# The first up-projection weights split during the last output products, and the last residual queued behind the first sums

## Chip, cores and metric

The kernel runs on one core of one Trainium2 chip. The metric is device time in microseconds (us); lower is better. A core has TensorE (PE in the profile, its weight loads PEld), VectorE (DVE), ScalarE (ACT), GpSimd (POOL) and SyncE (SP), which issues most of the DMAs. Each engine works off its own queue in order.

## What is computed

One inference step of a trunk of two layers, over 512 latent tokens and 128 context tokens of width 1024, in float32. Layer 0 mixes tokens by two-dimensional neighbourhood attention, layer 1 by grouped-query attention. After each mixer comes a gated convolutional feed-forward network (FFN). The parts around the change are these:

```python
xs = xs + g_as * rmsnorm(os_.reshape(bs, ts, -1) @ w_o, norm_mix_post[l])    # output products, residual
hs = rmsnorm(xs, norm_ffn_pre[l]) * (1.0 + sc_fs) + sh_fs                     # norm, scale and shift
fs = conv_ffn(hs, ffn_w_up[l], ffn_conv_w[l], ffn_conv_b[l], ffn_w_down[l])

def conv_ffn(h, w_up, conv_w, conv_b, w_down):
    u = h @ w_up                                            # 1024 -> 2 x 2816
    up = jnp.pad(u, ((0, 0), (1, 1), (0, 0)))
    u = up[:, :-2] * conv_w[0] + up[:, 1:-1] * conv_w[1] + up[:, 2:] * conv_w[2] + conv_b
    a, gt = jnp.split(u, 2, axis=-1)
    return (jax.nn.silu(a) * gt) @ w_down
```

The context tokens go the same way with their own g, sc and sh.

## The kernel before

**Numbers.** A float32 operand is split into a rounded high part (a copy on ACT) and a low part, the difference (a subtraction on DVE or POOL). A product is three matmuls: high with high, low with high, high with low. A weight goes through three kinds of buffers in the pool `wp`, four of each: `wr` (as loaded), `wh` and `wl` (its parts). A buffer is used again when its last reader is done, so a load or a split waits for that.

**Tiles.** The 640 tokens are five tiles of 128; tile 4 is the context. The output projection of the mixer (class `Mix`, from line 659) runs in two halves of 512 columns. `part0` makes the first halves `y0` of all tiles ahead; `second` (line 675) goes through the tiles and makes the second half `y1`, eight products (p = 0 to 7) per tile, with the four weights `ws[1, 0]` to `ws[1, 3]`, each for two values of p. Within the products of tile t, behind p = TP = 1, it issues the transposes of tile t-2, and the residual and the shift of tile t-1.

**Finish** (class from line 318) turns products into the FFN's input. `ahead` loads the modulation rows (`mod`) and the old residual (`xo`). `stat` squares and sums half a row on ACT (line 349) and lets POOL scale the sum (351); `rms` takes the power on POOL (358). `sums` multiplies the products by the gate on DVE (366 and 368) and gives the banks of the products back. `residual` adds to the old residual on DVE (378, two halves), stores it, takes squares again and multiplies by the norm's scale (387, two halves). `shifted` applies the root and the shift on DVE (393, two halves). `turns` transposes the tile on TensorE (117); the results are copied into `hF` and, for the first columns, split into the parts `B` (215, 216 on ACT, 220 on DVE).

**The FFN's beginning** (`ffn`, line 1063). The up-projection has 22 pairs of chunks, the value and the gate of 128 features. Most pairs are multiplied by a scheme that forms sums of blocks of the weights (lines 1132 to 1135) and of the columns (class `Halves`, line 194) and saves products. The first `PLAIN` = 2 pairs, four chunks, go the plain way, since the column sums are not there yet. `plain0` (line 1229) makes two products of twelve matmuls for one chunk, `ux` and `uy`, over the first 322 columns, which are ready first. It copies `ux` on ACT (1165), adds `uy` to the copy on DVE (1236) into the tile `C`, and gives the bank of `uy` back. `plain1` does the other columns later. Between the `plain0` of the second and the third chunk stand the transposes of tile 3, behind the fourth those of tile 4; then follow the two products of the next value weight, and `plain1` of the four chunks. `Halves.first` (line 233) makes column parts from `hF` (237 on DVE, 230 on ACT, 231 on DVE). `fetch` (1103) loads up to four weights ahead, one more for each that has been split; `split` makes the parts (1111 on ACT, 1112 on DVE or POOL). The low parts of the first two chunks are on POOL, those of the other two on DVE.

**The order.** TensorE's order is that of the program text (the helper `pe` chains its instructions). PSUM has eight banks, which the class `Banks` hands out first in, first out. On the other engines a planner at build time orders the instructions: what is traced first has the higher rank, and what it takes to be ready and ranks highest comes next. Each engine then keeps that order, whatever really is ready. An explicit edge (`tc.add_manual_dep`) fixes the order of two instructions.

Of the kernel before, what the change touches and what calls it, by code (L numbers as in the profile page):

```python
# [101 lines left out]
def hybrid_step(ctx: ExitStack, tc: tile.TileContext, A, O):  # L102
# [215 lines left out]
    class Finish:  # L318
# [27 lines left out]
        def stat(self, y, first=None):  # L346
            junk = self.np.tile([P, 512], BF16, tag="junk", name="junk")
            ss = sm.tile([P, 1], F32, name="sso", bufs=12)
            nc.scalar.activation(junk, y, AF.Square, accum_out=ss)
# [23 lines left out]
        def residual(self, t):  # L373

            xm, r = self.xm[t]
            xo = self.xo.pop(t)
            for c in HALF:
                nc.vector.scalar_tensor_tensor(xo[:, c], xm[:, c], r, xo[:, c], op0=ALU.mult, op1=ALU.add)
                if not self.nxt:
                    nc.sync.dma_start(self.xnew(t)[:, c], xo[:, c])  # L380
            if not self.nxt:
                return
            nc.sync.dma_start(self.xnew(t), xo)
            v = None
            for c in HALF:
                v = self.stat(xo[:, c], v)
                (nc.vector if v else nc.gpsimd).tensor_mul(xm[:, c], xo[:, c], self.gs[:, c])
            self.xm[t] = xm, self.rms(v)

        def shifted(self, t):  # L390
            xm, r = self.xm[t]
            for c in HALF:
                nc.vector.scalar_tensor_tensor(
                    xm[:, c], xm[:, c], r, self.sh[:, c], op0=ALU.mult, op1=ALU.add
                )

        def turns(self, t):
# [259 lines left out]


    class Mix:

# [13 lines left out]

        def second(self, fin):

# [377 lines left out]
    for t in range(NT):  # L1054
        m0.part0(t, 7)
    late = m0.second(fin)
    fin.close()
    r_na.close()
# [3 lines left out]

    def ffn(l, hT, hT_close, xold, xnew, nxt, todo, late, late_close, side, back, after=None):

# [27 lines left out]
        with ExitStack() as s2:  # L1092
            sw = s2.enter_context(pool("sw", 1, side))
            sw2 = s2.enter_context(pool("sw2", 2, side))
            ct = up = ada = None
            ws, raws, done = {}, {}, set()
            nr = [0]

# [64 lines left out]
            def copied(name, p, u):  # L1163
                small[name, p] = sw2.tile([P, TH], F32, tag=name, name=name)
                nc.scalar.copy(small[name, p], u)  # L1165

# [62 lines left out]
            def plain0(p, i):  # L1229

                x = banks["p", p, i] = bk.get("ux")
                block_product(x[:, 0:TH], ws[p, i], 0, "11", True)
                copied("c1", (p, i), x[:, 0:TH])
                y = bk.get("uy")
                block_product(y[:, 0:TH], ws[p, i], 1, "21", True)
                nc.vector.tensor_add(block(p, i, 0), y[:, 0:TH], small.pop(("c1", (p, i))))
                bk.put(y)

            def plain1(p, i):
# [27 lines left out]
            more = hT.sums()  # L1267
            hT.begin(sw, "234")
            next(more)
# [111 lines left out]
    def gqa_w(c0, u, low=None):  # L1381
# [4 lines left out]
        0, hT, hp1.close, lambda t: xres[0][t], lambda t: xres[1][t], (1, 1, 0, NS),  # L1386
        ((0, 5), (1, 1), (1, 0), (1, 2), (1, 4), (1, 3)), late, xmp.close, "right", "left",
        lambda u: wkv.append(gqa_w(1024, u)),
# [353 lines left out]
    late = m1.second(fin)  # L1742
    fin.close()
# [5 lines left out]
    _, _, _, xmp = ffn(  # L1749
        1, hT, r_h3.close, lambda t: xres[2][t], y_out, None, ((1, 5),), late, xmp.close, "left", "right"  # L1750
    )
# [70 lines left out]
```

## Time and profile before

| | us |
|---|---|
| median of 3 runs | 1609.09 (1608.65 to 1611.68) |
| profiled execution, its own time | 1610.03 |
| profiled execution, span of its instructions | 1608.2 |
| PE busy | 1541.6 |
| DVE busy | 1023.0 |
| ACT busy | 860.6 |
| POOL busy | 722.2 |

A row of the timeline reads: start in us from the span's start, duration in us, engine, line, operation, output<-inputs, shapes, count, and in brackets the idle time of the engine before it with what ended it. Several instructions in a row of one kind are merged (x2). A matmul's duration overlaps the next one's, so the pace is read from the distance of the starts. The output projection's second half of layer 0 ends with TensorE at 387.24 us, that of layer 1 at 1154.59; these two places are called the boundaries. The chunks, counted 0 to 3 in the order of `plain0`, follow from there.

### The profile page before, as it was taken

The numbers are of one execution on the slowest core, as the hardware profiler recorded it, in microseconds if no ns is written. First come the engines' busy times: TensorE is split into PE (matmuls) and PEld (weight loads), VectorE is DVE, ScalarE is ACT, GpSimd is POOL, SyncE is SP. The second block draws the span as 40 slices with busy tenths as digits, with TensorE's granted clock in tenths as the row PEclk, the third lists the DMA queues.
The fourth block names the chain that finished last, engine by engine and source line by source line (L and its number), as shares of the span: only waits on it lengthen the run. The fifth ranks groups of instructions, "written<-read, shape, count | busy, mean of one in ns | idle before, by whom it ended". The sixth has DMA issues, their size and how long they took to land.

```text
span 1608.2 us, 26065 instructions
## 1 busy us (share of the span) xinstructions
PE 1541.6 (96%) x9709; PEld 1360.4 (85%) x9709; DVE 1023.0 (64%) x1646; ACT 860.6 (54%) x1641; POOL 722.2 (45%) x613
## 2 busy tenths in 40 slices
PE   5999999899999999999999888999999999999998
PEld 3989899777999999988887666778899999998886
DVE  3453533538877666674656867774887888876554
ACT  3474655545565555554453536764555556565343
POOL 1554554324355445544443344441524565553433
PEclk8999999999999999999999998999999999999999
DMA  9745454236456566578573110004634333348664
GB/s 290 185 113 146 117 151 119 62 105 198 144 185 194 199 209 186 193 241 299 170 236 131 60 40 14 2 1 143 211 109 156 105 117 115 104 149 276 206 211 140
DMA packets 193211, 242.42 MB, mean 151 GB/s; under 512 B 11100, under 2 KB 149564, under 8 KB 193084
## 3 DMA queue, kind: packets, MB, share of 16 engines
q1 hardware_dynamic: 182224, 233.13, 45.4%
q10 hardware_dynamic: 10860, 7.62, 2.7%
q8 instruction: 76, 1.25, 0.3%
q14 instruction: 51, 0.42, 0.1%
HBM read 214.38 MB, written 26.34 MB: 150 GB/s over the span
## 4 chain that ended last, share of the span: by engine, by line
PE 73%; DVE 10%; POOL 6%; issue 4%; ACT 4%; DMA 2%; SPq 1%; ACTq 0%; POOLq 0%; DVEq 0%
PE acc L114 18%; PE ux L114 15%; PE y L114 7%; PE uz L114 6%; PE qk L114 5%; PE uy L114 4%; PE po L114 4%; PE s L114 4%; PE vp L114 3%; PE tp L117 3%; PE ada L114 2%; POOL wl L1112 1%; DVE al L1112 1%; POOL vl L1112 1%; DMA wf<-in_ada_w 1%
## 5 line engine op out<-in xcount | busy, mean ns | idle before, releaser
L167 POOL TENSOR_TENSOR wl<-wr,wh 128x1024 fp32r<-128x1024 f32 x74 | 181.5, 2455 | 263.4 <-ACT wh L165 255.2
L1112 POOL TENSOR_TENSOR wl<-wr,wh 128x1024 fp32r<-128x1024 f32 x80 | 194.2, 2448 | 46.1 <-ACT wh L1111 42.6
L114 PE MATMUL ux<-B,wh 128*128 128x322 f32 x832 | 201.9, 314 | 1.4 <-ACT u L1165 0.9
L1188 DVE SCALAR_TENSOR_TENSOR t<-C,cw,t 128x644 f32<-128x644 f32 x176 | 156.3, 888 | 49.1 <-ACT t L1186 48.4
L114 PE MATMUL acc<-wh,alo 128*128 128x512 f32 x440 | 172.3, 392 | 0.6 <-DVE alo L1081 0.6
L114 PE MATMUL acc<-wh,ahi 128*128 128x512 f32 x440 | 171.9, 391 | 0.0
L114 PE MATMUL acc<-wl,ahi 128*128 128x512 f32 x440 | 171.9, 391 | 0.0
L165 ACT CAST wh<-wr 128x1024 fp32r<-128x1024 f32 x140 | 145.5, 1048 | 33.5 <-DMA wr<-in_ffn_w_down 24.3
L114 PE MATMUL uz<-B,wh 128*128 128x322 f32 x640 | 156.5, 313 | 0.7 <-ACT v L1165 0.7
L114 PEld LDWEIGHTS ux<-B,wh 128*128 128x128 f32 x832 | 145.0, 190 | 4.3 <-ACT u L1165 1.2
L1081 DVE TENSOR_TENSOR alo<-ain,ahi 128x384 fp32r<-128x384 f32 (+1 forms) x88 | 77.3, 893 | 89.8 <-ACT ahi L1079 88.8
L114 PE MATMUL ux<-B,wl 128*128 128x322 f32 x416 | 130.1, 313 | 0.2
L114 PE MATMUL qk<-hT,wh 128*128 128x384 f32 (+1 forms) x512 | 122.8, 317 | 0.1
L114 PEld LDWEIGHTS uz<-B,wh 128*128 128x128 f32 x640 | 110.9, 188 | 3.6 <-ACT vh L1111 1.6
L1112 POOL TENSOR_TENSOR vl<-wr,vh 128x1024 fp32r<-128x1024 f32 x38 | 97.1, 2556 | 30.9 <-ACT vh L1111 30.5
L1111 ACT CAST wh<-wr 128x1024 fp32r<-128x1024 f32 x88 | 88.7, 1048 | 32.6 <-DVE wr L1135 31.4
L1186 ACT ACTIVATE t<-C,cw 128x644 f32<-128x644 f32 x88 | 78.6, 893 | 45.9 <-DVE C L1216 43.9
L114 PE MATMUL uz<-B,wl 128*128 128x322 f32 x320 | 99.5, 311 | 0.1
L167 DVE TENSOR_TENSOR wl<-wr,wh 128x1024 fp32r<-128x1024 f32 x66 | 84.5, 1293 | 23.6 <-ACT wh L165 23.1
L114 PEld LDWEIGHTS acc<-wh,alo 128*128 128x128 f32 x440 | 82.5, 188 | 19.1 <-DVE alo L1081 1.4
L1079 ACT CAST ahi<-ain 128x384 fp32r<-128x384 f32 (+1 forms) x88 | 40.1, 460 | 108.4 <-PE acc L114 91.4
L114 PEld LDWEIGHTS acc<-wl,ahi 128*128 128x128 f32 x440 | 82.6, 188 | 17.8
(249 smaller groups left out, 4010.2 us busy)
## 6 DMA issues: line engine op xcount, KB each, us to landing
wr<-in_ffn_w_up SPq DMA_DIRECT2D x88, 512.0 KB
wr<-in_ffn_w_down SPq DMA_DIRECT2D x88, 512.0 KB
wr<-in_ada_w SPq DMA_DIRECT2D x80, 512.0 KB
act<-act SPq DMA_DIRECT2D x44, 321.0 KB
wr<-in_na_w_qkv SPq DMA_DIRECT2D x24, 512.0 KB
mod<-modrow SPq DMA_DIRECT2D x20, 512.0 KB
ain<-act SPq DMA_DIRECT2D x44, 192.0 KB
wf<-in_ada_w SPq DMA_DIRECT2D x16, 512.0 KB
```

The source lines that it names most:

```text
L114: pe(nc.tensor.matmul(*a, **k))
L117: pe(nc.tensor.transpose(*a, **k))
L165: i = nc.scalar.copy(hi, raw)
L167: j = (low or nc.vector).tensor_sub(lo, raw, f32(hi))
L1079: pin(nc.scalar.copy(hi[:, 0 : c1 - c0], ain[:, 0 : c1 - c0]))
L1081: pin(nc.vector.tensor_sub(lo[:, 0 : c1 - c0], ain[:, 0 : c1 - c0], f32(hi[:, 0 : c1 - c0])))
L1111: nc.scalar.copy(hl[0], src)
L1112: low.tensor_sub(hl[1], src, f32(hl[0]))
L1186: nc.scalar.activation(t, taps(0), AF.Identity, bias=cw[:, 3, n : n + 1], scale=cw[:, 1, n : n + 1])
L1188: nc.vector.scalar_tensor_tensor(t, taps(d), cw[:, w, n : n + 1], t, op0=ALU.mult, op1=ALU.add)
```

## The change

The change has these parts, the same in both layers:

- The loads of the first two chunks' weights, and their splits, leave `ffn` and go into a small class `First`. The loads are traced ahead of `second`. The splits are traced inside it, in the products of tile 4: the first behind p = 1, the second behind p = 3, where the last products with `ws[1, 0]` and `ws[1, 1]` lie. Their low parts are on DVE, not on POOL.
- Edges on DVE put the residual of tile 3 behind the low part of the first split, and the shift of tile 3 behind that of the second.
- The residual and the shift of tile 4 leave the end of `second`. They are traced in `ffn`, behind the `plain0` of chunks 0 and 1 (`Finish.last`), with edges: the residual behind the sum (1236) of chunk 0, its first square on ACT behind the copy (1165) of chunk 1, the shift behind the sum of chunk 1.
- In `ffn` the split of chunk 2 is traced ahead of `plain0` of chunk 0, that of chunk 3 behind tile 4's shift.
- `Finish` is closed later, after the shift of tile 4. The column parts "22", "1", "2", "3" and "4" therefore get a pool of their own, `swb`, opened after that. In layer 1 `Finish` takes its memory on the right side of SBUF, not on the left.

TensorE's order stays as it is.

```diff
         def stat(self, y, first=None):
...
-            nc.scalar.activation(junk, y, AF.Square, accum_out=ss)
+            self.stat_ins = nc.scalar.activation(junk, y, AF.Square, accum_out=ss)
...
+        def last(self, copied, added):
+            behind(self.residual(NT - 1), added[0])
+            behind(self.first_stat, copied[1])
+            behind(self.shifted(NT - 1), added[1])
+            self.close()
...
+    class First:
+        def __init__(self, l):
+            self.raws, self.ws = {}, {}
+            for i in range(2):
+                raw = self.raws[0, i] = wp.tile([P, KC, P], F32, tag="wr", name="wr")
+                nc.sync.dma_start(raw, rows(A["ffn_w_up"][l], 0, 8, i * FC * P, P))
+
+        def split(self, i):
+            raw = self.raws[0, i]
+            hi, lo = self.ws[0, i] = [wp.tile([P, KC, P], F32R, tag=x, name=x) for x in ("wh", "wl")]
+            nc.scalar.copy(hi, raw)
+            return nc.vector.tensor_sub(lo, raw, f32(hi))
+
+    def behind(ins, other):
+        tc.add_manual_dep(ins.ins, other.ins.name, no_sync, reason="order")
...
-        def second(self, fin):
+        def second(self, fin, first):
...
                     if p == TP:
                         low = fin.turns(t - 2) if t >= 2 else None
-                        if low and t == NT - 1:
+                        if t == NT - 1:
                             low()
+                            behind(fin.residual(t - 1), first.split(0))
+                            continue
                         if t >= 1:
                             fin.residual(t - 1)
-                        if low and t < NT - 1:
+                        if low:
                             low()
                         if t >= 1:
                             fin.shifted(t - 1)
+                    elif t == NT - 1 and p == 3:
+                        i = first.split(1)
+                        behind(fin.shifted(t - 1), i)
                 fin.sums(t, self.y0[t], y1, v0[t])
-            fin.residual(NT - 1)
-            fin.shifted(NT - 1)
...
-    late = m0.second(fin)
-    fin.close()
+    first = First(0)
+    late = m0.second(fin, first)
     r_na.close()
...
-            ws, raws, done = {}, {}, set()
-            nr = [0]
+            ws, raws, done = first.ws, first.raws, set(first.ws)
+            nr = [len(raws)]
...
-            for n, c in enumerate(chunks):
-                plain(*c, nc.gpsimd if n < 2 else nc.vector)
-            hT.begin(sw, ("22", "1"))
-            for n, c in enumerate(chunks):
+            plain(*chunks[2], nc.vector)
+            fin0.last(*zip(*(plain0(*c) for c in chunks[:2])))
+            plain(*chunks[3], nc.vector)
+            swb = s2.enter_context(pool("swb", 1, side))
+            hT.begin(swb, ("22", "1"))
+            late[0]()
+            hT.first(0)
+            value(PLAIN, nc.vector)
+            for c in chunks[2:]:
                 plain0(*c)
-                if n == 1:
-                    late[0]()
-                    hT.first(0)
-                    value(PLAIN, nc.vector)
...
-    fin = Finish(1, 2, lambda t: xres[1][t], lambda t: xres[2][t], (1, 4, 3, NS + 1), hT, xmpool, 6)
+    fin = Finish(1, 2, lambda t: xres[1][t], lambda t: xres[2][t], (1, 4, 3, NS + 1), hT, xmpool, 6, "right")
```

`residual` and `shifted` return their first DVE instruction, `plain0` the copy and the sum, for these edges; layer 1 is called in the same way with `First(1)`.

More of the change, by code (lines that the diff above doesn't have):

```diff
@@ L376, in residual @@
             xo = self.xo.pop(t)
+            got = None
             for c in HALF:
-                nc.vector.scalar_tensor_tensor(xo[:, c], xm[:, c], r, xo[:, c], op0=ALU.mult, op1=ALU.add)
+                i = nc.vector.scalar_tensor_tensor(xo[:, c], xm[:, c], r, xo[:, c], op0=ALU.mult, op1=ALU.add)
+                got = got or i
                 if not self.nxt:
@@ L386, in residual @@
                 v = self.stat(xo[:, c], v)
+                if c is HALF[0]:
+                    self.first_stat = self.stat_ins
                 (nc.vector if v else nc.gpsimd).tensor_mul(xm[:, c], xo[:, c], self.gs[:, c])
             self.xm[t] = xm, self.rms(v)
+            return got
         def shifted(self, t):
             xm, r = self.xm[t]
-            for c in HALF:
+            return [
                 nc.vector.scalar_tensor_tensor(
@@ L395, in shifted @@
                 )
+                for c in HALF
+            ][0]
+        def last(self, copied, added):
[3 more added lines that the diff above has]
+            self.close()
         def turns(self, t):
@@ L1055, in hybrid_step, with ffn @@
         m0.part0(t, 7)
-    late = m0.second(fin)
-    fin.close()
+    first = First(0)
+    late = m0.second(fin, first)
     r_na.close()
-    def ffn(l, hT, hT_close, xold, xnew, nxt, todo, late, late_close, side, back, after=None):
+    def ffn(l, hT, hT_close, xold, xnew, nxt, todo, late, late_close, side, back, first, fin0, after=None):
         s = ExitStack()
@@ L1164, in copied @@
                 small[name, p] = sw2.tile([P, TH], F32, tag=name, name=name)
-                nc.scalar.copy(small[name, p], u)
+                return nc.scalar.copy(small[name, p], u)
             def sums(p):
@@ L1232, in plain0 @@
                 block_product(x[:, 0:TH], ws[p, i], 0, "11", True)
-                copied("c1", (p, i), x[:, 0:TH])
+                c = copied("c1", (p, i), x[:, 0:TH])
                 y = bk.get("uy")
                 block_product(y[:, 0:TH], ws[p, i], 1, "21", True)
-                nc.vector.tensor_add(block(p, i, 0), y[:, 0:TH], small.pop(("c1", (p, i))))
+                a = nc.vector.tensor_add(block(p, i, 0), y[:, 0:TH], small.pop(("c1", (p, i))))
                 bk.put(y)
+                return c, a
             def plain1(p, i):
@@ L1386, in hybrid_step @@
         0, hT, hp1.close, lambda t: xres[0][t], lambda t: xres[1][t], (1, 1, 0, NS),
-        ((0, 5), (1, 1), (1, 0), (1, 2), (1, 4), (1, 3)), late, xmp.close, "right", "left",
+        ((0, 5), (1, 1), (1, 0), (1, 2), (1, 4), (1, 3)), late, xmp.close, "right", "left", first, fin,
         lambda u: wkv.append(gqa_w(1024, u)),
@@ L1741, in hybrid_step @@
         m1.part0(t, 7)
-    late = m1.second(fin)
-    fin.close()
+    first = First(1)
+    late = m1.second(fin, first)
     l_o1.close()
@@ L1749, in hybrid_step @@
     _, _, _, xmp = ffn(
-        1, hT, r_h3.close, lambda t: xres[2][t], y_out, None, ((1, 5),), late, xmp.close, "left", "right"
+        1, hT, r_h3.close, lambda t: xres[2][t], y_out, None, ((1, 5),), late, xmp.close, "left", "right", first, fin
     )
```

2 lines of the change are left out of this document (1 added, 1 removed).

## The prediction

> **What bounds the kernel now.** I read the totals first, then TensorE's waits at the two places that the diff touches, then the chain and the DVE queue there. The totals of the page:
>
> ```profile
> span 1608.2 us, 26065 instructions
> PE 1541.6 (96%) x9709; PEld 1360.4 (85%) x9709; DVE 1023.0 (64%) x1646; ACT 860.6 (54%) x1641; POOL 722.2 (45%) x613
> ```
>
> TensorE bounds the whole, so a change off TensorE pays only where TensorE waits. Its waits from 380 to 480 us (layer 0) and from 1148 to 1250 us (layer 1), as engine, line and releaser, total, count, longest:
>
> ```profile
> PE uy L114 <- DVE C L1236: 3.2, 1, 3.2
> PE ux L114 <- DVE B L220: 0.2, 1, 0.2
> ```
>
> Both answers have these same two rows, and in the 100 us from the boundary on there is nothing else to win. The chain of waits behind each long one:
>
> ```profile
> 401.16 3.11 PE uy L114 x12
> 404.27 2.24 PE ux L114 x12
> 406.52 1.78 PE uy L114 x12
> ...
> 1168.51 2.57 PE uy L114 x12
> 1171.08 2.78 PE ux L114 x12
> ```
>
> TensorE's second product of the third chunk waits for a PSUM bank. Eight banks go round first in, first out; that one was freed by the sum C of chunk 0 (L1236), which stands on DVE behind tile 4's residual and shift and a weight split. And the wait is followed by slow products: twelve matmuls take 1.78 in the third row, 3.11 and 2.24 in the two before it, so 1.33 + 0.46 = 1.79 us more; in layer 1 0.79 + 1.00 = 1.79 too. The granted clock agrees (columns: length, PE, PEld, DVE, ACT, POOL busy with counts, clock, DMA):
>
> ```profile
> 382.15:412.01 29.86, 26.39 (x160) 24.75 (x159) 28.78 (x39) 17.39 (x34) 11.19 (x15) 0.94 0.39 124
> ...
> 400.00:406.00 6.00, 4.84 (x22) 4.84 (x23) 6.00 (x9) 4.55 (x8) 0.00 (x0) 0.72 0.30 89
> ```
>
> The clock is 0.72 in the slice that follows the wait. DVE is the other thing to see: 28.78 of 29.86 us busy, one wait of 1.08 in all. It is the local bound, and what the change does to it decides.
>
> **The change part by part.** First what TensorE could gain. Rows of its timeline:
>
> ```profile
> 387.24 0.31 PE L114 MATMUL ux<-B,wh 128*128 128x322 f32 x1
> 395.16 1.04 PE L117 MATMUL tr<-ident,xm 128*128 128x128 f32 x8
> 395.96 0.40 PE L114 MATMUL ux<-B,wh 128*128 128x322 f32 x1
> 412.55 0.31 PE L114 MATMUL ux<-B,wh 128*128 128x322 f32 x1
> ```
>
> From the first row (chunk 0) to the last (the first product after the four chunks) lie 25.31 us. The work in it is ten products of twelve matmuls at 1.78 and two sets of transposes at 0.80 (395.16 to 395.96): 19.40. So 5.91 are lost: 3.2 in the wait, 1.79 in the clock, 0.2 in the short wait, and some 0.7 in pauses between products. I leave 0.16 of those to the change between transposes and products, twice 0.08, so at most 5.75 can come back per boundary.
>
> *The residual and shift of tile 4 behind the sums.* DVE rows now, in order:
>
> ```profile
> 383.35 3.55 DVE L378 SCALAR_TENSOR_TENSOR xo<-xm,ro,xo 128x512 f32<-128x512 f32 x2
> 387.43 0.42 DVE L220 TENSOR_TENSOR B<-tr,B 128x264 fp32r<-128x264 f32 x1
> 389.32 3.50 DVE L393 SCALAR_TENSOR_TENSOR xm<-xm,ro,mod 128x512 f32<-128x512 f32 x2
> 392.74 1.21 DVE L1112 TENSOR_TENSOR wl<-wr,wh 128x1024 fp32r<-128x1024 f32 x1
> 393.87 0.68 DVE L368 TENSOR_TENSOR xm<-y,mod 128x512 f32<-128x512 f32 x1
> 394.47 1.40 DVE L378 SCALAR_TENSOR_TENSOR xo<-xm,ro,xo 128x512 f32<-128x512 f32 x2
> 395.80 1.28 DVE L387 TENSOR_TENSOR xm<-xo,mod 128x512 f32<-128x512 f32 x2
> 398.16 1.41 DVE L393 SCALAR_TENSOR_TENSOR xm<-xm,ro,mod 128x512 f32<-128x512 f32 x2 [1.08 <-POOL ro L358]
> 399.49 1.22 DVE L1112 TENSOR_TENSOR wl<-wr,wh 128x1024 fp32r<-128x1024 f32 x1
> 400.63 0.88 DVE L1236 TENSOR_TENSOR C<-uy,c 128x322 f32<-128x322 f32 x2
> ```
>
> No instruction is added: the sums pass in front. Nothing but tile 4's transposes, ahead of the last two of the ten products, waits for residual and shift, and the DMA of the new residual (issued on SP) is read a whole FFN later.
>
> *The first two splits.* Their low parts leave POOL, where they are these rows, and go to DVE; the high parts are on ACT now, the first as soon as a weight buffer comes free, and stay there:
>
> ```profile
> 382.42 1.05 ACT L1111 CAST wh<-wr 128x1024 fp32r<-128x1024 f32 x1 [0.64 <-PE y L114]
> 384.87 0.66 ACT L349 ACTIVATE junk<-xo 128x512 bf16<-128x512 f32 x1
> ...
> 383.55 2.81 POOL L1112 TENSOR_TENSOR wl<-wr,wh 128x1024 fp32r<-128x1024 f32 x1 [0.55 <-ACT wh L1111]
> 389.18 2.41 POOL L1112 TENSOR_TENSOR wl<-wr,wh 128x1024 fp32r<-128x1024 f32 x1
> ```
>
> DVE pays 2 x 1.14 us (392.74 to 393.87, 399.49 to 400.63). But a pair L378 and a pair L393 took 3.55 and 3.50 while these POOL rows ran, and 1.40 and 1.41 with POOL idle, so 2.15 + 2.09 come back: DVE is relieved by 1.96, and by its 1.08 wait at 398.16 if that is filled. If the slowness of the pairs has another cause, DVE gets 2.28 heavier instead; nothing else on POOL or ACT overlaps both, so I take the relief.
>
> *DVE in the new order*, counted by distances between starts in these rows (0.60 for L368 and L366, 1.33 for a pair L378 or L393, 1.20 for a pair L387, 0.35 for L220, 0.40 for a sum). From 383.4, where residual 3 begins now and the first high part is done: low part 0 384.6, the two L220 385.3, residual 3 386.6, its L387 387.8, low part 1 388.9, L366 389.5, shift 3 390.9, L368 391.5, low part 2 392.6, sum 0 393.0, residual 4 394.3, L387 395.5, sum 1 395.9, low part 3 397.1, the 1.08 wait, shift 4 399.5. TensorE meanwhile: chunks 0 and 1 387.24 to 394.36, transposes to 395.16, chunk 2's second product 396.9 (sum 0 long done: the 3.2 is gone), chunk 3 at 398.7 (needs sum 1 and low part 3: margins 2.8 and 1.7), transposes of tile 4 at 402.3 (shift 4: margin 2.8). There DVE is short. Before tile 4's transposes are through it has the first column parts, the next weight's low part and two more sums, in rows
>
> ```profile
> 401.43 0.94 DVE L237 TENSOR_TENSOR hF<-hF 128x760 f32<-128x760 f32 x1
> 404.02 1.80 DVE L231 TENSOR_TENSOR B<-hF,B 128x760 fp32r<-128x760 f32 x2
> 406.15 0.68 DVE L1132 TENSOR_TENSOR wr<-wr 128x512 f32<-128x512 f32 x1
> 410.77 1.32 DVE L231 TENSOR_TENSOR B<-hF,B 128x528 fp32r<-128x528 f32 x2
> ```
>
> 0.87 + 1.73 + 1.13 + 0.40 bring it from 399.5 to the sum of chunk 2 at 403.6, and by the round of banks the second half of those transposes (402.7) takes the bank that this sum frees. I take 1.2 us of TensorE waiting there: bounds 0 (that sum is put ahead of the low part) and 2.5 (two of the four 0.6 us block sums of L1132 and its like stand ahead of it). So 5.75 - 1.2 = 4.55, taken as 4.5 per boundary.
>
> On the clock: one wait of 3.2 us cost 1.79, 0.56 per us, so 1.2 us of waiting might cost another 0.67 per boundary. The Trainium skill (TensorE: Matmul & The Clock Gate, Part 1: The HAM clock gate) says that the clock halves only after an idle window of about 3.4 us. The trace is near it: 3.2 idle and then a clock of 0.72. By that rule a wait of 1.2 costs nothing more and the sum below stands; by the row in proportion the gain would be 1.3 us smaller. Neither changes which case is likeliest.
>
> *The added orders.* Residual 3 on DVE now waits for low part 0, and with it L387, shift 3 and the sums of tile 4. If ACT copies tile 2's transposes before it rounds the high part, low part 0 comes some 1.5 us later (today these four copies lie between the two ACT rows above); shift 3 is done at 390.9 and needed at 394.4, so that is hidden. On ACT tile 4's first square waits for the copy of chunk 1 (near 393.3, when its first product ends), while residual 4's first half ends near 393.7: nothing. The sums also need C, whose edges POOL clears. In layer 1 that clearing waits for shift 4 today:
>
> ```profile
> 1166.97 0.13 POOL L1171 MEMSET C<- 128x3 f32 x2 [1.46 <-DVE xm L393]
> ```
>
> If that were for memory it would now be a circle, as shift 4 waits for a sum; with the modulation tiles on the other side of SBUF C no longer lies where they were, and I cost it at nothing.
>
> *The loads.* The two weight DMAs are traced ahead of the modulation and residual loads. On SP now (the second weight load waits for POOL):
>
> ```profile
> 350.16 0.82 SPq L331 DMA_DIRECT2D mod<-modrow  x2
> ...
> 354.19 5.75 SPq L1103 DMA_DIRECT2D wr<-in_ffn_w_up  x2
> ```
>
> If the order holds, it costs nothing: 354.19 is when their buffers come free. The later pool of column parts and the other side for layer 1's tiles only change which released memory is waited for. No row prices that; I take 0, between nothing and the 1.08 of one DVE wait.
>
> **The sum.** 2 x 4.5 = 9.0 off the span of 1608.2 gives 1599.2. The profiled execution took 1610.03, 1.83 more than its span, so 1601.0; it lies 0.94 above the median of 1609.09, so **1600.1** against the median.
>
> **The rivals.** A difference under 0.2% (3.2 us) is about what a measurement of this kernel cannot tell from none.
>
> *DVE sets the pace.* If DVE keeps its fill (block sums, low parts of later weights) ahead of the last column parts (410.77 + 1.32), the products at 412.55 move only as far as DVE does: 1.96 to 3.04, say 2.5 a boundary, 1604.1. For it: DVE is full from 400 to 412. Against it: the fill, four L1132-like steps and two half splits of 0.6 each, 3.6 us, is traced later and needed later.
>
> *The wait stays.* The edges put residual 4 behind sum 0, yet nothing puts sum 0 ahead of low parts or block sums; if these stay in front, the wait shrinks by about 1 and with the small waits 1.5 a boundary comes back, 1606.1. Against it: these are traced after or cost 1.14 each.
>
> *Slower: the loads in the wrong order.* If the two weight loads are queued ahead of the rest, SP holds the modulation and residual loads until 359.95 (354.19 + 5.75) instead of 350.16, 9.8 later. The first use of the modulation is an L366 at 357.44, at most 7.3 after its load; with that lag it would start at 367.2, and after two L366, L368 and the root (1.2 + 0.7 + 0.9) residual 0 would start near 369.9 instead of 364.5:
>
> ```profile
> 357.44 1.27 DVE L366 TENSOR_TENSOR xm<-y,mod 128x512 f32<-128x512 f32 x2
> 364.52 1.41 DVE L378 SCALAR_TENSOR_TENSOR xo<-xm,ro,xo 128x512 f32<-128x512 f32 x2 [0.40 <-POOL ro L358]
> 367.95 1.42 DVE L393 SCALAR_TENSOR_TENSOR xm<-xm,ro,mod 128x512 f32<-128x512 f32 x2 [0.81 <-POOL ro L358]
> 369.38 1.03 PE L117 MATMUL tr<-ident,xm 128*128 128x128 f32 x8
> ```
>
> Tile 0's transposes follow its shift with no slack (369.37, 369.38), so TensorE would wait 5.4, and lose 1.79 in the clock: 7.2 against 4.5, +2.7 a boundary, 1614.5. It decides from a shift of 2.7 on. Against it: the modulation loads head the queue today and wait there for memory.
>
> **How the numbers follow.** Forecast 0.55, DVE sets the pace 0.20, the wait stays 0.12, slower 0.13. Faster by over 0.2% are the first two with a little of the third, 0.76; within 0.2% 0.11; slower 0.13. The forecast alone runs from full recovery (2 x 5.75, 1597.6) to 2.5 us of waiting with a proportional clock (2 x 1.85, 1605.4). With the wait that stays taken in to beyond its value, the range is 1597.5 to 1608.5; outside are the slower case and little else.
>
> **What would show it.** Right: no wait for C L1236 among TensorE's waits at either boundary, the clock at 1.00 in those slices, pairs L378 and L393 all near 1.4, both low parts on DVE ahead of their chunks, and 20 to 22 us instead of 25.31 from chunk 0 to the product that is now at 412.55. Wrong: a new wait over 2.5 us at tile 4's transposes or the next weight (DVE sets the pace), mod loads behind weight loads on SP with a wait ahead of tile 0's transposes, or a gain there that TensorE's later waits in the FFN hand back; today these have none up to 480 us.

## The result, and the profile after

The changed kernel takes 1602.05 us (median of 5 runs, 1601.49 to 1603.20); beside it the kernel before took 1609.96 (5 runs, 1608.65 to 1611.68). The ratio is 0.9949, 95% interval 0.9936 to 0.9962: faster by 7.9 us. The profiled execution took 1601.92 with a span of 1600.1, 8.1 less than the 1608.2 of before. The same kernel was timed twice more beside other experiments, with ratios of 0.9960 (0.9948 to 0.9973) and 0.9956 (0.9942 to 0.9969). One of the eleven executions of the experiment e2 below took 3246.36 us, twice the others; its ratio leaves that one out, and no run shows the reason.

The line numbers of the code have moved: the residual is L379 now (378 before), its scaling L391 (387), the shift L398 (393), the splits L1146 and L1147 (1111 and 1112), the sum L1271 (1236). The low parts of chunks 0 and 1 are L686, in `First`.

The totals of the page after:

```profile
span 1600.1 us, 26043 instructions
PE 1537.8 (96%) x9709; PEld 1357.3 (85%) x9709; DVE 1023.9 (64%) x1650; ACT 859.8 (54%) x1641; POOL 710.9 (44%) x609
```

POOL has four instructions less, DVE four more: the low parts of two chunks in two layers. All of TensorE's waits after, from 380 to 480 us and from 1148 to 1250 us (total, count, longest):

```profile
PE ux L114 <- DVE wl L1147: 1.4, 1, 1.4
...
PE ux L114 <- DVE wl L1147: 1.3, 1, 1.3
```

The wait of 3.2 us for the sum C is gone in both layers. In its place stands a shorter one, for the low part of chunk 3. The chain of waits at the two boundaries after (start, duration, what):

```profile
397.82 1.42 DVE xm L398 x2
399.24 1.14 DVE wl L1147
...
400.42 1.90 PE ux L114 x11
402.32 1.78 PE uy L114 x12
...
404.54 0.66 PE tr L117 x4
...
1162.48 1.15 DVE wl L1147
...
1163.67 1.89 PE ux L114 x11
```

The low part stands behind tile 4's shift on DVE, and TensorE goes on as soon as it ends. The eleven matmuls behind the wait take 1.90 to the end of the last, the next twelve 1.78 as undisturbed ones do. The stretches behind the waits, with the granted clock as the eighth number of the row (after the five engines' busy times with their counts):

```profile
400.00:406.00 6.00, 5.58 (x38) 5.33 (x39) 6.00 (x9) 3.03 (x7) 0.00 (x0) 1.00 0.31 91
1161.00:1167.00 6.00, 4.73 (x32) 4.48 (x31) 5.93 (x7) 2.03 (x4) 0.03 (x1) 1.00 0.40 128
```

Before, the clock in 400 to 406 was 0.72; it is 1.00 now. DVE's queue after, in its order (start, duration, engine, line, operation, output<-inputs, count, and in brackets the idle time ahead of it):

```profile
383.40 0.75 DVE L379 SCALAR_TENSOR_TENSOR xo<-xm,ro,xo 128x512 f32<-128x512 f32 x1
...
385.95 1.22 DVE L686 TENSOR_TENSOR wl<-wr,wh 128x1024 fp32r<-128x1024 f32 x1
387.08 0.75 DVE L379 SCALAR_TENSOR_TENSOR xo<-xm,ro,xo 128x512 f32<-128x512 f32 x1
387.74 1.22 DVE L686 TENSOR_TENSOR wl<-wr,wh 128x1024 fp32r<-128x1024 f32 x1
...
390.64 1.42 DVE L398 SCALAR_TENSOR_TENSOR xm<-xm,ro,mod 128x512 f32<-128x512 f32 x2 [1.08 <-POOL ro L358]
...
392.59 1.21 DVE L1147 TENSOR_TENSOR wl<-wr,wh 128x1024 fp32r<-128x1024 f32 x1
393.72 0.48 DVE L1271 TENSOR_TENSOR C<-uy,c 128x322 f32<-128x322 f32 x1
394.13 1.40 DVE L379 SCALAR_TENSOR_TENSOR xo<-xm,ro,xo 128x512 f32<-128x512 f32 x2
...
396.65 0.48 DVE L1271 TENSOR_TENSOR C<-uy,c 128x322 f32<-128x322 f32 x1
397.82 1.42 DVE L398 SCALAR_TENSOR_TENSOR xm<-xm,ro,mod 128x512 f32<-128x512 f32 x2 [0.69 <-POOL ro L358]
399.15 1.22 DVE L1147 TENSOR_TENSOR wl<-wr,wh 128x1024 fp32r<-128x1024 f32 x1
...
404.00 0.48 DVE L1271 TENSOR_TENSOR C<-uy,c 128x322 f32<-128x322 f32 x1
```

The first sum stands ahead of tile 4's residual now, at 393.72 (before, the first two stood behind the shift, at 400.63). The pairs of L379 and L398 take 1.40 and 1.42 where 3.55 and 3.50 stood. The row of the residual's group over the whole execution, one instruction each (least, median, longest in ns), after, says the same for both layers:

```profile
L379 DVE SCALAR_TENSOR_TENSOR xo<-xm,ro,xo x40: 734/746/754, 364.4 to 1595.9; 128x512 f32<-128x512 f32 x40
```

In the kernel before, the same group reads

```profile
L378 DVE SCALAR_TENSOR_TENSOR xo<-xm,ro,xo x40: 735/746/2891, 364.5 to 1604.5; 128x512 f32<-128x512 f32 x40
```

Where the time came from is read on TensorE's timeline, after:

```profile
387.12 0.30 PE L114 MATMUL ux<-B,wh 128*128 128x322 f32 x1
...
400.42 0.41 PE L114 MATMUL ux<-B,wl 128*128 128x322 f32 x1 [1.40 <-DVE wl L1147]
...
403.94 1.26 PE L117 MATMUL tr<-ident,xm 128*128 128x128 f32 x8
404.95 0.40 PE L114 MATMUL ux<-B,vh 128*128 128x322 f32 x1
...
408.59 0.31 PE L114 MATMUL ux<-B,wh 128*128 128x322 f32 x1
...
424.59 0.31 PE L114 MATMUL uz<-B,wh 128*128 128x322 f32 x1
```

From chunk 0 to the first product after the four chunks it takes 408.59 - 387.12 = 21.47 us instead of 25.31. The work in it is still 19.40, so 2.07 are lost instead of 5.91: the wait of 1.40, 0.21 at tile 4's transposes (403.94 to 404.95 is 1.01 where the undisturbed set took 0.80), and 0.46 in pauses.

For the experiments I use a longer stretch, from chunk 0 to the first matmul into `uz`, so that a wait put off to the products right after is still in it. It ends with the last row above: 424.59 - 387.12 = 37.47 us. In the kernel before it is 41.32 (layer 0) and 41.33 (layer 1), after 37.47 and 37.35. Of the 8.1 us of span, 3.85 + 3.98 = 7.83 come from these two stretches. The nine products added take 16.0 us at 1.78, so the work in the stretch is 35.4.

### The profile page after: what moved, and what is told of

Its sections match the earlier page's. It is cut to its first block, busy times and chain, and to the rows that moved or that the text cites. A ratio compares the mean times of both kernels' runs of the same rounds, so it can differ in the third digit from the quotient of the medians.

```text
span 1600.1 us, 26043 instructions
## 1 busy us (share of the span) xinstructions
PE 1537.8 (96%) x9709; PEld 1357.3 (85%) x9709; DVE 1023.9 (64%) x1650; ACT 859.8 (54%) x1641; POOL 710.9 (44%) x609
## 4 chain that ended last, share of the span: by engine, by line
PE 55%; DVE 9%; POOL 5%; ACT 3%; issue 3%; DMA 1%; ACTq 0%; POOLq 0%; DVEq 0%
PE acc L114 18%; PE ux L114 15%; PE uz L114 6%; PE uy L114 4%; PE y L114 2%; PE s L114 2%; PE po L114 2%; PE tp L117 2%; PE ada L114 2%; POOL wl L1147 1%; DVE t L1223 1%; POOL vl L1147 1%; DVE al L1147 1%; POOL rh L1467 1%; DVE wl L167 1%
## 5 line engine op out<-in xcount | busy, mean ns | idle before, releaser
L167 POOL TENSOR_TENSOR wl<-wr,wh 128x1024 fp32r<-128x1024 f32 x74 | 183.1, 2476 | 261.7 <-ACT wh L165 252.3
L1147 POOL TENSOR_TENSOR wl<-wr,wh 128x1024 fp32r<-128x1024 f32 x76 | 183.5, 2437 | 39.5 <-ACT wh L1146 35.9
L165 ACT CAST wh<-wr 128x1024 fp32r<-128x1024 f32 x140 | 145.3, 1048 | 40.7 <-DMA wr<-in_ffn_w_down 30.9
L1147 POOL TENSOR_TENSOR vl<-wr,vh 128x1024 fp32r<-128x1024 f32 x38 | 96.3, 2534 | 24.6 <-ACT vh L1146 24.3
L1146 ACT CAST wh<-wr 128x1024 fp32r<-128x1024 f32 x84 | 84.9, 1049 | 40.9 <-DVE wr L1170 40.5
L114 PEld LDWEIGHTS acc<-wh,ahi 128*128 128x128 f32 x440 | 82.6, 188 | 17.8
```

The costliest lines, as they stand in the source:

```text
L114: pe(nc.tensor.matmul(*a, **k))
L165: i = nc.scalar.copy(hi, raw)
L167: j = (low or nc.vector).tensor_sub(lo, raw, f32(hi))
L1146: nc.scalar.copy(hl[0], src)
L1147: low.tensor_sub(hl[1], src, f32(hl[0]))
```

## The experiments

Line numbers differ a little between these kernels; the operation and the names tell which instruction it is. A table first, of all kernels. "Stretch" is from chunk 0 to `uz` in layers 0 and 1; "beside before" is the median minus that of the kernel before on the same chip.

| kernel | stretch, us | median, us | beside before | ratio, 95% interval |
|---|---|---|---|---|
| before | 41.32, 41.33 | 1609.96 | | |
| changed | 37.47, 37.35 | 1602.05 | -7.9 | 0.9949 (0.9936 to 0.9962) |
| changed, second time | 37.47, 37.38 | 1603.56 | -5.9 | 0.9960 (0.9948 to 0.9973) |
| changed, third time | 37.48, 37.36 | 1603.20 | -7.9 | 0.9956 (0.9942 to 0.9969) |
| e1: tile 4 early again | 41.11, 40.68 | 1610.65 | +0.6 | 1.0002 (0.9993 to 1.0011) |
| e2: low parts on POOL again | 39.67, 40.20 | 1608.81 | -1.3 | 0.9992 (0.9983 to 1.0001) |
| e3: low part 3 ahead of shift 4 | 39.45, 39.50 | 1608.95 | -1.2 | 0.9993 (0.9982 to 1.0005) |
| e5: weight loads first on SP | 37.96, 37.35 | 1607.98 | -2.1 | 0.9988 (0.9980 to 0.9997) |
| e4: weight loads behind on SP | 37.47, 37.37 | 1602.74 | -6.7 | 0.9956 (0.9943 to 0.9968) |
| e7: sums ahead too | 37.71, 37.63 | 1603.45 | -6.0 | 0.9962 (0.9950 to 0.9975) |
| e8: no edges on tile 3 | 37.49, 37.53 | 1603.55 | -5.9 | 0.9960 (0.9947 to 0.9974) |
| e9: rounding and column parts behind too | 39.75, 40.28 | 1609.84 | -1.3 | 0.9994 (0.9985 to 1.0004) |

The stretch repeats within 0.03 us for the changed kernel, the whole time within 2. In the three profiles of the changed kernel, chunk 0 of layer 0 starts at 387.12, 387.47 and 389.29: its whole time varies ahead of the change. So differences of 2 us and less between whole times are not used below; the stretch is.

My theory was that of the prediction: the wait for C and the slow clock behind it are what comes back, by two things that add up on DVE, the new order and the end of the slow pairs. The rivals: one of the two does it alone; DVE sets the pace; the loads cost something.

### e1: without the new place of tile 4

```diff
+            fin.residual(NT - 1)
+            fin.shifted(NT - 1)
+            fin.close()
...
-            fin0.last(*zip(*(plain0(*c) for c in chunks[:2])))
+            for c in chunks[:2]:
+                plain0(*c)
```

The first three lines stand at the end of `second`, as before. The splits stay in `First`, with their low parts on DVE, and the edges on tile 3 stay too.

> The changed kernel, with the residual and shift of tile 4 back at the end of the output products, without their edges; the first splits stay inside the output products with their low parts on DVE. Theory A (the order of tile 4 against the sums and later low parts is what pays): DVE again does tile 4 first, then low part 2, then the sums; low part 2 then ends near 399.3 in layer 0 where TensorE wants it near 395.2, so TensorE waits 3 to 4 us at each boundary, with slow products behind it; 1608 to 1612 us. Theory B (the lighter DVE, without POOL's splits in its way, is what pays): 1602 to 1604 us, like the changed kernel (1602.05).

Measured: 1610.65, no gain, as theory A said. TensorE's timeline and then its stretch in this kernel:

```profile
399.14 0.42 PE L114 MATMUL ux<-B,wl 128*128 128x322 f32 x1 [3.43 <-DVE wl L1150]
```

```profile
400.00:406.00 6.00, 6.00 (x33) 6.00 (x32) 5.74 (x7) 1.26 (x2) 0.00 (x0) 0.72 0.61 176
```

There is no wait for C, but one of 3.43 us for the low part of chunk 2, which stands behind tile 4's residual and shift on DVE, and the clock falls to 0.72 as before. Without the order, the low parts on DVE (and the early loads and splits with them) give 0.2 and 0.65 us: the order is needed.

### e2: the order alone, low parts on POOL

```diff
-            return nc.vector.tensor_sub(lo, raw, f32(hi))
+            return nc.gpsimd.tensor_sub(lo, raw, f32(hi))
...
-                            behind(fin.residual(t - 1), first.split(0))
+                            fin.residual(t - 1)
+                            first.split(0)
...
-                        i = first.split(1)
-                        behind(fin.shifted(t - 1), i)
+                        fin.shifted(t - 1)
+                        first.split(1)
```

The edges on tile 3 go as well here; e8 takes them out alone.

> The changed kernel with the first two low parts on POOL and without the two edges of tile 3; the order of tile 4 stays. Theory A (order pays, the engine of the low parts pays little): the pairs of tile 3 on DVE take 3.5 us again, DVE is 1.96 later per boundary, and this comes on top of the 1.4 us wait that is left: 1603 to 1606 us. Theory B (the lighter DVE is what pays): most of the 8 us is gone, 1607 to 1610 us.

Measured: 1608.81, the time of theory B; the interval of its ratio reaches just beyond 1. DVE's timeline, and POOL's, in this kernel:

```profile
385.15 3.55 DVE L379 SCALAR_TENSOR_TENSOR xo<-xm,ro,xo 128x512 f32<-128x512 f32 x2
...
391.11 3.50 DVE L398 SCALAR_TENSOR_TENSOR xm<-xm,ro,mod 128x512 f32<-128x512 f32 x2
```

```profile
385.34 2.81 POOL L686 TENSOR_TENSOR wl<-wr,wh 128x1024 fp32r<-128x1024 f32 x1 [0.55 <-ACT wh L685]
...
390.98 2.41 POOL L686 TENSOR_TENSOR wl<-wr,wh 128x1024 fp32r<-128x1024 f32 x1
```

The pairs are back at 3.55 and 3.50 us. The second starts at 391.11, POOL's subtraction ends at 393.39, and the pair is done when DVE's next instruction starts at 394.53: 1.14 us later, where two halves alone take 1.33, so that in the main both ran after POOL's end. In the first pair, the half that started ahead of POOL ran at once, the other behind it. That settles the step of the prediction that could have gone the other way: the slowness came from POOL's subtractions. With DVE this late, TensorE waits for C in other places, in short waits that leave the clock at 1.00 (waits of this kernel, 360 to 440 us):

```profile
PE tr L117 <- DVE C L1272: 1.4, 1, 1.4
PE ux L114 <- DVE C L1272: 0.5, 1, 0.5
PE uy L114 <- DVE C L1272: 0.4, 1, 0.4
```

The order alone brings the stretch down by 1.65 and 1.13 us, the low parts on DVE alone by 0.21 and 0.65, both by 3.85 and 3.98. The two do not add up: together they give about twice the sum. Each alone leaves something on DVE too late for TensorE.

### e3: the low part of chunk 3 ahead of tile 4's shift

The 1.40 us that are left are a wait for a low part that the planner put behind the shift. This kernel puts it ahead, as the prediction had it.

```diff
-            behind(self.shifted(NT - 1), added[1])
+            i = self.shifted(NT - 1)
+            behind(i, added[1])
+            behind(i, low)
...
-            fin0.last(*zip(*(plain0(*c) for c in chunks[:2])))
-            plain(*chunks[3], nc.vector)
+            ca = [plain0(*c) for c in chunks[:2]]
+            fin0.last(*zip(*ca), plain(*chunks[3], nc.vector))
```

> The changed kernel with low part 3 ahead of tile 4's shift on DVE (one edge more). The wait of 1.4 us that TensorE has left at each boundary is for low part 3, which stands behind a shift that waits for POOL. Theory A (only this order costs it): the wait goes, and 1.0 to 1.4 us per boundary come back: 1599.3 to 1600.2 us. Rival (DVE as a whole is the bound there): the wait moves on to tile 4's transposes, whose second half waits for the sum of chunk 2, and at most 0.5 per boundary comes back: 1601 to 1602 us.

Measured: 1608.95, and 39.45 in the stretch: 2.0 us more than the changed kernel, where both sides had expected a little less. TensorE's timeline, its stretch and the chain in this kernel:

```profile
404.86 1.12 PE L117 MATMUL tr<-ident,xm 128*128 128x128 f32 x4 [2.28 <-DVE C L1274]
```

```profile
404.54:407.95 3.41, 3.09 (x13) 3.09 (x14) 3.41 (x7) 1.77 (x3) 0.00 (x0) 0.50 0.02 5
```

```profile
405.98 2.71 PE ux L114 x12
```

The wait for the low part is gone, and the wait that the prediction had forecast has come up: the second half of tile 4's transposes needs the bank that the sum of chunk 2 frees. It takes 2.28 us, and now the clock drops to 0.50 for 3.41 us: twelve matmuls take 2.71 instead of 1.78, the four transposes 0.77 (404.86 to the next product at 405.63) instead of 0.40, 1.3 us together. In the changed kernel the 1.40 us wait ahead of it hides this one: there the sum is done when DVE's next instruction starts at 404.41, and TensorE takes the second half at 404.54.

### e5 and e4: the weight loads ahead of and behind the others

The slower rival of the prediction said that the two weight loads, queued ahead on SP, would hold the modulation and the residual back. In the changed kernel's own SP queue half of that has happened (SP's timeline after):

```profile
350.05 0.81 SPq L331 DMA_DIRECT2D mod<-modrow  x2
354.08 2.63 SPq L680 DMA_DIRECT2D wr<-in_ffn_w_up  x2
356.76 1.04 SPq L343 DMA_DIRECT2D xo<-in_x_sample  x2
```

Two modulation rows still go ahead, but the old residual is issued at 356.76, behind the weights, and residual 0 still starts at 364.39 (before 364.52). e5 forces the weights ahead of everything that `ahead` loads for the first two tiles:

```diff
-            nc.sync.dma_start(t, modrow[l][i][cond].partition_broadcast(P))
+            i = nc.sync.dma_start(t, modrow[l][i][cond].partition_broadcast(P))
+            if self.front:
+                behind(i, self.front)
```

and the same for the load of `xo`; `self.front` is the second weight load.

> The changed kernel with the two weight loads forced ahead of all modulation and residual loads on SP. Price by the prediction's slower rival: the first modulation tile comes some 7 to 10 us later, tile 0's residual starts up to 5.4 us later and TensorE waits at tile 0's transposes: up to 7.2 us more per boundary, 1609 to 1616 us. Other theory (in the changed kernel the residual loads already start 5.7 us later and nothing moves, so there is slack): within 1601 to 1604 us, tile 0's transposes start when they did.

Measured: 1607.98, between the two ranges expected. SP's timeline, and TensorE's, in this kernel:

```profile
354.07 2.62 SPq L685 DMA_DIRECT2D wr<-in_ffn_w_up  x2
356.78 2.66 SPq L332 DMA_DIRECT2D mod<-modrow  x3
```

```profile
372.40 1.32 PE L117 MATMUL tr<-ident,xm 128*128 128x128 f32 x8 [2.99 <-DVE xm L403]
```

TensorE waits 2.99 us at tile 0's transposes, as the rival had it, the clock falls (0.74 in the 3 us behind), and chunk 0 starts at 392.11 instead of 387.12; in layer 1 the wait is only 0.3. So the rival's mechanism exists, at some 5 us in layer 0, and takes most of the gain back. It did not decide because the first modulation rows kept their place.

e4 traces the weight loads behind those of `ahead` instead. The two loads go from `First`'s constructor into a function of their own, which `second` calls behind its first calls of `ahead`:

```diff
+        def load(self):
+            l = self.l
...
+            first.load()
```

> The changed kernel with the two weight loads traced behind the loads of the first two residuals; on SP the residual loads then go out ahead of them again, as in the kernel before, the later modulation loads still behind. If the order of loads in the changed kernel costs nothing: the same time within 1.5 us, tile 0's transposes at the same place.

Measured: 1602.74, a stretch of 37.47 and 37.37 as in the changed kernel. The place that the change gave the loads costs nothing that can be measured.

### e7: the sums ahead of the column parts too

If low part 3 goes ahead, the sum of chunk 2 must not stand behind column differences. e7 is e3 with

```diff
+            behind(hT.subs[0], sa[0])
...
-                    corner(PLAIN)
+                    behind(corner(PLAIN), sa[1])
```

`hT.subs[0]` is the first column difference, `sa` holds the sums of chunks 2 and 3, and `corner(PLAIN)` gives a later low part.

> Low part 3 ahead of tile 4's shift as in the run before, and two more edges: the sum of chunk 2 ahead of the first column difference, the sum of chunk 3 ahead of the next half split. Theory (with low part 3 ahead, TensorE waits at tile 4's transposes because their second half takes the bank that the sum of chunk 2 frees; that 2.3 us wait also slows the clock): with the sum in front both waits go, the clock stays at 1.00, and the stretch from chunk 0 to the first product into uz shrinks from 37.4 to about 35.8 us, 3 us less than the changed kernel in all, near 1599 us. Rival (DVE as a whole is late, whatever its order): a wait of 1 us or more turns up at the next weight or at the next column parts, and the time is that of the changed kernel or more.

Measured: 1603.45, a stretch of 37.71 and 37.63: as good as the changed kernel, not better: the theory's 1599 missed, and the time is the rival's. TensorE now waits 0.7 us for a sum at 406, and 0.7 for a copy at 429, behind the stretch. What holds the sums is on ACT (the timelines of ACT and of DVE in this kernel):

```profile
401.49 0.62 ACT L1148 CAST ah<-wr 128x512 fp32r<-128x512 f32 x1 [2.99 <-DMA wr<-in_ffn_w_up]
402.02 0.42 ACT L1203 COPY c<-ux 128x322 f32<-128x322 f32 x1
```

```profile
402.47 0.49 DVE L1274 TENSOR_TENSOR C<-uy,c 128x322 f32<-128x322 f32 x1 [0.73 <-ACT c L1203]
```

A rounding waits 2.99 us for its load and holds the copy behind it. DVE waits 0.73 us for that copy with the sum of chunk 2, and everything behind it comes later, the sum of chunk 3 too.

### e8: without the edges on tile 3

```diff
-                            behind(fin.residual(t - 1), first.split(0))
+                            fin.residual(t - 1)
+                            first.split(0)
...
-                        i = first.split(1)
-                        behind(fin.shifted(t - 1), i)
+                        fin.shifted(t - 1)
+                        first.split(1)
```

> The changed kernel without the two edges of tile 3 (residual behind low part 0, shift behind low part 1); both low parts stay on DVE. If these edges do nothing for TensorE: the low part of chunk 0 comes some 1.7 us later, about 0.5 us after TensorE wants it, and the time is that of the changed kernel or up to 1 us more. If they are what keeps the first chunks fed: TensorE waits over 1 us at chunk 0 or 1, and 2 us or more are lost.

Measured: 1603.55, a stretch of 37.49 and 37.53. As the first side had said, nothing is lost: TensorE waits 0.9 us for the low part of chunk 3 and 0.3 for one of the first two, instead of 1.4. These two edges move a wait and win nothing.

### e9: the rounding and the last column parts behind as well

e9 adds to e7 what held its sum: on ACT the rounding goes behind the copy of chunk 3, on DVE the early column part "1" behind the sum of chunk 3, and the next low part and the large column difference behind the last of these parts (`hT.ones`). The lines stand against e7; `self_hi[0]` is the rounding, `sc[1]` the copy.

```diff
-            nc.vector.tensor_sub(b12, b22, b12)
+            behind(nc.vector.tensor_sub(b12, b22, b12), self.ones[1])
...
+            behind(hT.ones[0], sa[1])
...
-                    behind(corner(PLAIN), sa[1])
+                    behind(corner(PLAIN), hT.ones[1])
...
+            behind(self_hi[0], sc[1])
```

> The variant with the sums ahead, and four more orders: the second corner split's rounding on ACT (it waits for a weight load) behind the copy of chunk 3; the first column part "1" behind the sum of chunk 3; the corner's low part and the first column difference of all columns behind the last of the early column parts. Theory (what is left of the waits at the boundary is made by orders: in the variant before, the copy of chunk 2 stood on ACT behind a rounding that waited 3.0 us for its load, and the sum behind that copy): the stretch from chunk 0 to uz goes from 37.7 to 36.0 to 36.5 us, with TensorE's own work 35.4, and 2 to 3 us less than the changed kernel in all. Rival (DVE's total work there is the floor): 37.4 again, same time as the changed kernel.

Measured: 1609.84, a stretch of 39.75 and 40.28, slower than either side had said. Up to 420.8 us TensorE waits for nothing at all. Then, in the waits of this kernel from 360 to 480 us:

```profile
PE ux L114 <- ACT wh L1150: 1.8, 1, 1.8
PE ux L114 <- DVE wl L1151: 1.0, 1, 1.0
```

Both are for the next weight. DVE forms its block sums late (DVE's timeline in this kernel):

```profile
421.15 0.68 DVE L1175 TENSOR_TENSOR wr<-wr 128x512 f32<-128x512 f32 x1
...
423.07 2.35 DVE L1151 TENSOR_TENSOR wl<-wr,wh 128x1024 fp32r<-128x1024 f32 x2
```

In the changed kernel these low parts start at 419.05. So what was put back on DVE comes due 15 us later, and the two waits together slow the clock again (0.50 from 425.17 to 428.58). Which of the four added orders costs this was not taken apart. No order tried here takes the last 1.4 us away; e3, e7 and e9 only choose the place, and no version has a shorter stretch than the changed kernel.

## Why the prediction was right, and where it was not

**The time.** 1600.1 was forecast, 1602.05 measured, within the range. Against the profile's own time it was 1601.0 forecast, 1601.92 measured; the gain was 7.8 us in the two stretches instead of 9.0 (whole times beside the kernel before: 7.9, 5.9 and 7.9).

**The wait for C and the clock: right.** The wait of 3.2 and the 1.79 behind it are gone at both boundaries, the clock is 1.00 there. e1 shows that the order is needed for it.

**The relief of DVE: right in its cause.** The pairs are back at 1.4 with POOL idle (longest L379 754 ns, before 2891) and at 3.5 when e2 puts the subtractions back. But it is worth more than the 1.96 us that it gives DVE: without it (e2) the order yields 1.65 and 1.13 instead of 3.85 and 3.98.

**DVE in the new order: wrong in one place, and the remaining wait with it.** This is the step that failed. I had the low part of chunk 3 end at 397.1, ahead of the shift of tile 4, with a margin of 1.7. It is traced behind the shift, and the planner kept that: it ended at 400.29, 0.69 us of idle time for the root and the whole shift ahead of it. So the margin of 1.7 became a wait of 1.40. The wait of 1.2 that I forecast, at tile 4's transposes, is 0.2. The sum of chunk 2 was done at 404.41 against 403.6 forecast; TensorE came late enough, by its 1.40, to meet it. Its size was loose from the start: by the prediction's own rows the sum comes 0.9 behind the time at which it is wanted (403.6 against 402.7), 2.1 with two block sums of 0.6 more, and the 1.2 and 2.5 taken there stand on no row. The limit by the round of banks was real: e3, with the low part where I had it, has the wait at those transposes, 2.28 us, nearer to my upper bound of 2.5 than to 1.2. I had the right two limits in reach and the wrong one first; that the total came out near is partly luck, since the one hides the other.

**The size.** 4.5 per boundary became 3.85 and 3.98. The difference in layer 0, 0.71 between 21.47 and my 25.31 - 4.55 = 20.76, is 0.20 more in the wait, 0.21 at the transposes, and 0.30 more of pauses than the 0.16 I left.

**The clock.** In proportion, 1.40 us of waiting would have cost 0.78; it cost nothing. The prediction's 0.56 per us was the wrong measure: a wait brings on a stretch at half the clock (3.41 us long behind each wait of 3.2, so some 1.7 us of work lost), or it costs nothing, as the last section shows. The Trainium skill (TensorE: Matmul & The Clock Gate, Part 1: The HAM clock gate) says that the clock halves after an idle window of about 3.4 us. The wait of 1.40 agrees with that; e3 goes against it, as an idle time of 2.28 slowed the clock.

**The added orders and the loads: nothing, as costed.** e8 and e4 agree. The edge on tile 3's residual binds one of its two halves only: the other went at 383.40, ahead of the low part at 385.95. The clearing of C in layer 1 made no wait.

**The rivals.** *DVE sets the pace* did not come true as a time (1604.1), but what is left points to it: DVE is busy 6.00 of 6.00 us in 400 to 406, and in e9 the wait comes back elsewhere. That DVE's work is the floor is not shown. *The wait stays* did not happen: sum 0 went ahead at 393.72. *Slower by the loads* was priced at 7.2 a boundary; forced, it cost some 5 in layer 0 and the wait of 0.3 in layer 1, so 1614.5 was too high even for its own case.

**What stays open.** Between whole times and the two stretches up to 2.5 us are not placed (e3 saves 3.7 in the stretches and 1.2 in the median). Part of it is the clock in other places: of the three profiles of the changed kernel, the one with chunk 0 at 389.29 has the half clock from 62.30 to 65.71, where the two others have the full clock. Nor was it tried to make DVE's work in these 40 us smaller, which is what e9 points to. There is some to win: in the changed kernel a column difference on DVE, at 410.28, takes 3.41 us beside a POOL subtraction that starts at 409.93, and 1.49 in the kernel before, where it starts ahead of POOL's and the hold falls on a later instruction; in e9 it takes 3.30.

## What to carry to other kernels

When a wait is removed by reordering a full engine, list that engine's queue anew with every instruction at its place by the planner's own rule (here, the order of the trace), and look at the two next limits, not one: here each hides the other, and moving the first away made the kernel slower. Work moved off a second engine can be worth more than its own duration, where that engine blocks the full one; take both edits out singly before crediting either. Price a wait of TensorE by whether it brings on a stretch of half clock, not in proportion to its length. And read short gains from a stretch between two fixed instructions, which repeated to 0.03 us here where the whole time moved by 2.

## What the runs showed of the hardware

**The clock falls by windows, not in proportion to a wait.** In the profiles of all twelve runs the granted clock is either 1.00 or 0.50, and its changes lie on a grid of 3.41 us whose place differs from execution to execution. A value such as 0.72 is a mean: 3.41 of 6 us at half the clock give 1 - 0.5 x 3.41 / 6 = 0.72. From 100 us on, each execution was divided along its own grid, and the windows at full clock were sorted by TensorE's idle time in them. After none of the 2565 with up to 1.72 us idle did the clock fall; after all of the 46 with 1.92 or more it did; after 9 of the 12 between, with 1.74 to 1.82, it did. So about half a window idle is enough. Two such windows, in the changed kernel around its wait of 1.40 (3.41 - 2.01 idle) and in e3 around its wait of 2.28 (3.41 - 1.46 = 1.95 idle), the second followed by the row of half clock shown with e3:

```profile
398.47:401.88 3.41, 2.01 (x14) 1.75 (x13) 3.41 (x5) 1.44 (x2) 0.00 (x0) 1.00 0.04 12
401.12:404.53 3.41, 1.46 (x11) 1.22 (x10) 3.01 (x4) 2.98 (x6) 0.00 (x0) 1.00 0.01 5
```

Short waits in one window count together: in e9 1.82 and 0.98 leave 1.23 us of work in the window that ends at 425.16, and the clock is 0.50 behind it. A wait that the grid cuts in two can cost nothing: one of 1.77 us for a transpose in layer 1 (it ends at 890.26 in the changed kernel, at 892.17 in e3, there 1.76 long) is followed by the half clock in e3 only.

**A subtraction on POOL holds DVE's instruction for its whole length.** A pair on DVE that reads two operands from SBUF took 1.40 alone and 3.50 to 3.55 beside a POOL subtraction of 2.41 to 2.81 us (e2). The ends agree with a lock, not with sharing: 393.39 for POOL, 1.14 later for the pair. It works the other way round too: in the kernel before, a POOL subtraction that starts at 413.88, just behind a DVE subtraction at 413.82, takes 5.10 us (2.41 to 2.81 in the pairs above). The Trainium skill (SBUF — State Buffer, SBUF: two separate sides) describes such an exclusive lock on a shared port pair, and the runs agree.

**Unexpected, but of the planner:** two things that save 0.2 to 0.65 and 1.1 to 1.65 us singly save 3.9 together.
